# Encoder trunk on one core: three stage boundaries rearranged (a transposition bank for one gate product, the first statistics, the odd mixer's constant rows)

## The chip, the cores and the metric

The kernel runs on one core of a Trainium2 chip. The core has five engines with a queue of instructions each: TensorE (PE, matrix products), VectorE (DVE), ScalarE (ACT), GpSimd (POOL) and SyncE (SP, which here only issues DMAs). Each engine works through its queue in order; semaphores make an instruction wait for another engine or a DMA. The metric is device time in microseconds (us) of one execution, lower is better. Every time in this text is in us unless it says otherwise.

## The reference

The reference is a two-layer encoder on 512 tokens of width 1024, all in fp32:

```python
for i in range(DEPTH):                       # DEPTH = 2
    h = h + 0.5 * swiglu(rmsnorm(h, norm_ffn1[i]), ffn1_w_gate[i], ffn1_w_up[i], ffn1_w_down[i])
    hn = rmsnorm(h, norm_mix[i])
    if i % 2 == 0:
        h = h + ab_mixer(hn, ...)            # windowed and dilated attention
    else:
        h = h + c_mixer(hn, ...)             # 2-D neighbourhood attention, 16 heads of 64
    h = h + 0.5 * swiglu(rmsnorm(h, norm_ffn2[i]), ffn2_w_gate[i], ffn2_w_up[i], ffn2_w_down[i])
    gate = jax.nn.sigmoid(rmsnorm(h, norm_ple[i]) @ w_ple_gate[i])
    h = h + gate * (p[i] @ w_ple_proj[i])    # per-layer input embedding
return rmsnorm(h, norm_final)
```

`rmsnorm` multiplies by `rsqrt(mean(x*x) + 1e-6)` and a gain; `swiglu` is `(silu(x @ w_gate) * (x @ w_up)) @ w_down` with 2816 inner columns. In the odd layer's mixer the 512 tokens are a grid 64 wide, and each query sees 8 rows by 16 columns around it.

## The kernel before, in words

**Layout.** The residual stream lies transposed: eight chunks (`KC = 8`) of 128 features by 512 tokens (`T = 512`). A weight *unit* is 128x1024 values, the weights of one block of 128 outputs over all eight chunks.

**Products.** An fp32 product is made of three matmuls (`mm3`, L175 to L177): high part by high part, high weight by low data, low weight by high data. A unit is loaded by SP into one of five raw buffers (`wr`), ACT copies its high part into `wh` (L150) and DVE subtracts to get the low part `wl` (L151), four buffers each. So a product of one unit over 512 tokens is 24 matmuls into one PSUM bank.

**PSUM.** There are eight banks in four pools: three `mm` (`bank`), two `sc` (`sbank`), two `tr` (`tbank`, for transpositions, column sums and the spread of the norm factor) and one `ob` (`obank`). A pool gives its banks out in turn; a new use waits for the readers of the old one.

**Norms.** The products run on the unnormalised data times the gain, and the factor 1/rms is multiplied in afterwards. ACT squares each chunk (L219), DVE adds the squares up (L226), PE sums over the partitions by products with a column of ones (`stat`, L233), DVE scales (L235), POOL takes the power -1/2 (L236), PE spreads the result over all partitions by four transposes (`spread`, L252), and ACT copies it into the tile `R` (L260). `rcol` and `R` are properties: whoever asks first puts that work at this place of the program.

**Stages.** Each layer runs FFN 1, the mixer, FFN 2 and the embedding stage (`ple`). In the FFN, `pair_front` makes the first four pairs of gate and up products (L294 to L297 are what follows them), `pair` the fifth, and a faster scheme (L390 to L392 on PE) the others. The first FFN of the program is special: it starts while x is still loading. For its first pair (m == 0) the units of the second pair are asked for ahead (`self.ahead`), then all eight squares and sums are issued, and R.

**The embedding stage** has eight chunks. The first three gate products are made ahead of R: m = 0 and m = 1 in `mm` banks with their projections in `ob` and `sc`, then m = 2 in the third `mm` bank (`ahead`); rcol and R come in the middle and at the end of it. From m = 3 on a gate product takes the next `mm` bank, and its projection (6 matmuls) an `sc` bank. DVE multiplies the gate by R (L1387), ACT takes the sigmoid (L1388), DVE multiplies with the projection (L1389) and adds to the stream (L1395 or L1412).

**The odd mixer** (`c`) starts with four sets of constant rows: eight tiles (`sel`, `low`) of which half the partitions hold a constant (64x512), brought by four DMAs into temporary tiles (L1201) and rounded by POOL (L1203). Then come the first q and k, the first v (`project_v`, L759 to L761, L778), and a weave of *steps* (the softmax and the P-V product of each of the sixteen heads, two to a pair) and *fill* (the projections of later pairs). L705 and L717 are ACT's copies that stack q and k by halves; q's are then copied by DMA into the free half of `sel` (L1233). L1301 are the scores, L1311 and L1317 the exponential and the normalisation, L791 the transposes of P, L801 and L802 the P-V product.

**What sets the order.** The program is written in one order, and a planner puts the instructions of each engine in the order in which, by its own costs, they can start. `issue_after` makes an instruction start behind a named one, `keep_in_program_order` ties a list, and `high_priority` draws a block ahead.

Of the kernel before, what the change touches and what calls it, by code (L numbers as in the profile page):

```python
# [15 lines left out]
P = 128  # L16
# [17 lines left out]
FRONT = 4  # L34
WHOLE = 4
# [13 lines left out]
class Trunk:  # L49
# [99 lines left out]
    def split(self, src, hi, lo, lo_eng=None):  # L149
        self.put(self.nc.scalar.activation(hi, src, AF.Copy))  # L150
        self.put((lo_eng or self.nc.vector).tensor_tensor(lo, src, hi.bitcast(F32), op=ALU.subtract))  # L151
# [64 lines left out]
    def norm_square(self, c):  # L216
        nc = self.nc
        sq = self.tmp() if c else self.small("ssq", [P, T], bufs=1)
        ins = nc.scalar.activation(sq, self.h[c], AF.Square)  # L219
        if self.k == 0:  # L220
            self.tc.keep_in_program_order(ins)
        if c == 0:
            self.acc = sq
        else:
            eng = nc.vector if c == KC - 1 or self.k in (0, 1, 3, 5, 7) else nc.gpsimd
            self.last_sum = eng.tensor_tensor(self.acc, self.acc, sq, op=ALU.add)  # L226

# [36 lines left out]
    def pair_front(self, w, m, first, ahead):  # L264

        nc = self.nc
        pgu = [self.bank(), self.sbank()]
        for j in range(2):
            u = self.ahead.pop(0) if self.ahead else self.unit(
                w[:, (1 - j) * UNIT:(2 - j) * UNIT], behind=self.last_sum if first and m == 2 else None)  # L270
            if not (first and m == 0):
# [12 lines left out]
        if m == 0 and first:  # L284

            with ExitStack() as s:
                for ins in self.last:
                    s.enter_context(self.tc.issue_after(ins.ins))
                self.ahead = [self.unit(ahead[:, (1 - j) * UNIT:(2 - j) * UNIT]) for j in range(2)]
            for c in range(KC):  # L290
                self.norm_square(c)
# [8 lines left out]
    def mm_pair(self, p, u, xs, j, ks=range(KC)):  # L300

        for k in ks:
            c = (k + KC // 2 * j) % KC * P
            self.mm3(p, (u[0][:, c:c + P], u[1][:, c:c + P]), xs[k], k == 0, k == KC - 1)
# [886 lines left out]
    def c(self, k_next):  # L1191
# [5 lines left out]
        for hf in range(2):  # L1197
            free = slice((1 - hf) * HD, (2 - hf) * HD)
            for name, dst in (("sel_c", sel), ("mask_c", low)):
                t = self.tmp()  # L1200
                nc.sync.dma_start(t[free, :], io[name])  # L1201
                for i in range(2):
                    nc.gpsimd.tensor_copy(dst[i][hf][free, :], t[free, :])  # L1203
# [52 lines left out]
        vs[0] = self.project_v(io["v_c"][0], nat, lambda: self.rcol, banks=[self.sbank(), self.bank()])  # L1256
        fill, steps = [], []
# [87 lines left out]
    def ple(self, i, k_next, regroup):  # L1345
# [4 lines left out]
        for m in range(KC):  # L1350
# [23 lines left out]
            for x in (slice(0, T // 2), slice(T // 2, T)) if half else (slice(0, T),):  # L1374
# [3 lines left out]
                else:  # L1378
                    pg, pp = (ahead if m == 2 else self.bank())[:, x], self.sbank()[:, x]
# [210 lines left out]
```

## Time and profile before

| | us |
|---|---|
| median of 3 runs | 2018.9 |
| lowest, highest | 2018.16, 2019.87 |
| profiled execution, its own time | 2018.84 |
| its span, first to last instruction | 2017.0 |
| PE busy | 1995.4 (99%) |
| DVE busy | 1593.9 (79%) |
| ACT busy | 1126.0 (56%) |
| POOL busy | 271.2 (13%) |

The granted clock of PE was 0.998 over the span. In a timeline each row gives the start, the length, the engine, the line and operation, output and inputs with their shapes, the count of merged instructions, and in brackets the idle time ahead of it with what ended it. A matmul's row is longer than the step to the next, since they overlap; the step is read from the starts. In a table of waits a row gives who waited for whom, the total in us, the number of times, and the longest.

### The profile page before, as it was taken

The page shows a single profiled execution, that of the slowest core. Times are in us where ns is not written, and L with a number is a line of the kernel's source. Part 1 is how long each engine was busy: PE and PEld are TensorE (multiplying, and loading weights), DVE is VectorE, ACT ScalarE, POOL GpSimd, SP SyncE. Part 2 cuts the span into 40 slices and gives each one's busy share as a digit, 9 for nine tenths or more (in the row PEclk, how much of TensorE's full clock was granted, in tenths as well). Part 3 has the DMA queues.
Part 4 walks back from the last instruction along what each step waited for, and adds up shares of the span by engine and source line. Part 5 has one row for each costly group of instructions (what it writes and reads, how often), then busy time and mean ns, then how long its engine had stood idle before and what let it go on. Part 6 is the DMA issues. An engine that isn't in the chain of part 4 may idle for free.

```text
span 2017.0 us, 33409 instructions
## 1 busy us (share of the span) xinstructions
PE 1995.4 (99%) x12438; PEld 1782.9 (88%) x12438; DVE 1593.9 (79%) x2803; ACT 1126.0 (56%) x1954; POOL 271.2 (13%) x314
## 2 busy tenths in 40 slices
PE   9999999999999999999999999999999999999997
PEld 6999988878888899988788999888988889998886
DVE  7888976798766888896778888958888678889675
ACT  6455655477644455575554555745766545556543
POOL 0000021342212000012120000113000100001211
PEclk9999999999999999999999999999999999999999
DMA  6666697643425466689554666885343446667971
GB/s 198 178 186 180 199 210 216 177 94 75 102 71 167 115 177 185 172 226 220 197 167 126 184 178 183 228 203 186 105 133 103 157 115 165 178 180 213 222 229 42
DMA packets 134963, 334.94 MB, mean 166 GB/s; under 512 B 24592, under 2 KB 32272, under 8 KB 134800
## 3 DMA queue, kind: packets, MB, share of 16 engines
q1 hardware_dynamic: 106944, 245.72, 36.0%
q0 software_dynamic: 27712, 87.05, 24.4%
q8 instruction: 98, 1.61, 0.3%
q14 instruction: 65, 0.53, 0.1%
q10 hardware_dynamic: 144, 0.04, 0.0%
HBM read 304.42 MB, written 17.27 MB: 159 GB/s over the span
## 4 chain that ended last, share of the span: by engine, by line
PE 75%; DVE 3%; ACT 2%; issue 1%; DMA 0%; POOL 0%; DVEq 0%; ACTq 0%; POOLq 0%
PE mm L176 5%; PE mm L175 5%; PE mm L177 5%; PE mm L391 5%; PE mm L392 5%; PE mm L390 5%; PE sc L390 2%; PE sc L392 2%; PE sc L391 2%; PE mm L511 2%; PE mm L509 2%; PE mm L510 2%; PE sc L175 2%; PE sc L177 2%; PE sc L176 2%; PE sc L511 1%
## 5 line engine op out<-in xcount | busy, mean ns | idle before, releaser
L150 ACT ACTIVATE wh<-wr 128x1024 fp32r<-128x1024 f32 (+2 forms) x435 | 447.9, 1031 | 428.0 <-PE mm L176 75.6
L151 DVE TENSOR_TENSOR wl<-wr,wh 128x1024 fp32r<-128x1024 f32 (+2 forms) x435 | 521.2, 1200 | 158.1 <-ACT wh L150 154.9
L390 PE MATMUL mm<-act,wh 128*128 128x256 f32 x1088 | 307.9, 283 | 0.0
L392 PE MATMUL mm<-act,wl 128*128 128x256 f32 x1088 | 307.9, 283 | 0.0
L391 PE MATMUL mm<-act,wh 128*128 128x256 f32 x1088 | 307.9, 283 | 0.0
L175 PE MATMUL mm<-act,wh 128*128 128x512 f32 (+1 forms) x632 | 248.0, 394 | 2.4 <-DVE tmp L1387 2.0
L176 PE MATMUL mm<-act,wh 128*128 128x512 f32 (+1 forms) x632 | 247.3, 392 | 0.7 <-DVE act L214 0.6
L177 PE MATMUL mm<-act,wl 128*128 128x512 f32 (+1 forms) x632 | 246.5, 391 | 0.0
L390 PEld LDWEIGHTS mm<-act,wh 128*128 128x128 f32 x1088 | 208.9, 192 | 0.2
L391 PEld LDWEIGHTS mm<-act,wh 128*128 128x128 f32 x1088 | 208.9, 192 | 0.2
L392 PEld LDWEIGHTS mm<-act,wl 128*128 128x128 f32 x1088 | 208.9, 192 | 0.0
L392 PE MATMUL sc<-act,wl 128*128 128x256 f32 x544 | 154.0, 283 | 0.0
L390 PE MATMUL sc<-act,wh 128*128 128x256 f32 x544 | 154.0, 283 | 0.0
L391 PE MATMUL sc<-act,wh 128*128 128x256 f32 x544 | 154.0, 283 | 0.0
L368 POOL DMA_DIRECT2D wr<-in_gu_dram x68 | 59.2, 870 | 677.2 <-DMA wr<-in_gu_dram 272.2
L175 PEld LDWEIGHTS mm<-act,wh 128*128 128x128 f32 x632 | 118.8, 188 | 26.0 <-DVE tmp L1387 2.9
L176 PEld LDWEIGHTS mm<-act,wh 128*128 128x128 f32 x632 | 118.9, 188 | 24.5 <-DVE act L214 3.3
L177 PEld LDWEIGHTS mm<-act,wl 128*128 128x128 f32 x632 | 118.9, 188 | 21.3
L500 POOL DMA_DIRECT2D wr<-in_dn_dram x80 | 69.2, 873 | 405.8 <-DVE wl L151 278.2
L151 DVE TENSOR_TENSOR act<-act,act 128x512 fp32r<-128x512 f32 (+1 forms) x176 | 108.3, 628 | 8.1 <-ACT act L150 5.6
L150 ACT ACTIVATE act<-act 128x512 fp32r<-128x512 f32 (+1 forms) x176 | 98.5, 577 | 16.9 <-DVE act L151 6.7
L390 PEld LDWEIGHTS sc<-act,wh 128*128 128x128 f32 x544 | 104.5, 192 | 0.0
(254 smaller groups left out, 4864.9 us busy)
## 6 DMA issues: line engine op xcount, KB each, us to landing
wr<-in_gu_dram SPq DMA_DIRECT2D x176, 512.0 KB, 4.2
wr<-in_gu_dram POOLq DMA_DIRECT2D x68, 512.0 KB, 5.4
wr<-in_dn_dram POOLq DMA_DIRECT2D x64, 512.0 KB, 7.1
tmp<-in_dn_dram SPq DMA_DIRECT2D x120, 256.0 KB, 4.7
rb<-in_gu_dram SPq DMA_DIRECT2D x68, 256.0 KB, 2.5
wr<-in_dn_dram SPq DMA_DIRECT2D x32, 512.0 KB, 4.6
act<-kept SPq DMA_DIRECT2D x56, 256.0 KB, 5.2
wr<-in_qk_ab_dram SPq DMA_DIRECT2D x20, 512.0 KB, 3.5
```

What stands on the lines that cost most here:

```text
L150: self.put(self.nc.scalar.activation(hi, src, AF.Copy))
L151: self.put((lo_eng or self.nc.vector).tensor_tensor(lo, src, hi.bitcast(F32), op=ALU.subtract))
L175: mm(out, stat[0], mov[0], start=start, stop=False)
L176: mm(out, stat[0], mov[1], start=False, stop=False)
L177: return mm(out, stat[1], mov[0], start=False, stop=stop)
L368: nc.gpsimd.dma_start(rs, w[:, :UNIT], accum_op=ALU.add)
L390: mm(out, w[0][:, c], xs[k][0][:, x], start=start and k == 0, stop=False, skip_group_check=True)
L391: mm(out, w[0][:, c], xs[k][1][:, x], start=False, stop=False, skip_group_check=True)
L392: mm(out, w[1][:, c], xs[k][0][:, x], start=False, stop=stop and k == half - 1, skip_group_check=True)
L500: nc.gpsimd.dma_start(raw, b[:, u.start * T:u.stop * T], accum_op=ALU.add)
L509: mm(p, xh, wh, start=start and k == 0, stop=False, skip_group_check=True)
L511: ins = mm(p, xl, wh, start=False, stop=stop and k == u.stop - 1, skip_group_check=True)
```

## The change

There are three edits.

**First statistics.** Of the second pair's units only the gate's is asked for ahead of the squares; the up unit's split is put behind the last square. The squares of the chunks behind `SQ_FIRST = 4` are tied behind the gate unit's high part. The second pair's gate product is started inside the first call of `pair_front` in two halves of 12 matmuls, with rcol between them and R behind the second; the second call takes it over (`self.started`).

**Embedding stage.** The gate product of m == 3 takes a `tr` bank.

**Odd mixer.** The constants are loaded and rounded behind the first v, by ACT.

```diff
@@ split, norm_square, mm_pair: what they keep or return
-        self.put(self.nc.scalar.activation(hi, src, AF.Copy))
+        self.last_hi = self.put(self.nc.scalar.activation(hi, src, AF.Copy))
...
+        return ins
...
-            self.mm3(p, (u[0][:, c:c + P], u[1][:, c:c + P]), xs[k], k == 0, k == KC - 1)
+            self.last_mm = self.mm3(p, (u[0][:, c:c + P], u[1][:, c:c + P]), xs[k], k == 0, k == KC - 1)
@@ pair_front
-        pgu = [self.bank(), self.sbank()]
+        pgu = [None if first and m == 1 else self.bank(), self.sbank()]
...
-            if not (first and m == 0):
+            if first and m == 1 and j == 0:
+                pgu[0] = self.started
+            elif not (first and m == 0):
                 self.mm_pair(pgu[j], u, self.xg, j)
...
-                self.ahead = [self.unit(ahead[:, (1 - j) * UNIT:(2 - j) * UNIT]) for j in range(2)]
+                self.ahead = [self.unit(ahead[:, UNIT:])]
+                hi = self.last_hi
             for c in range(KC):
-                self.norm_square(c)
+                with self.tc.issue_after(hi.ins) if c > SQ_FIRST else ExitStack():
+                    square = self.norm_square(c)
+            self.ahead.append(self.unit(ahead[:, :UNIT], behind=square))
+            self.started, half = self.bank(), KC // 2
+            self.mm_pair(self.started, self.ahead[0], self.xg, 0, range(half))
+            with self.tc.issue_after(self.last_mm.ins):
+                self.rcol
+            self.mm_pair(self.started, self.ahead[0], self.xg, 0, range(half, KC))
+            with self.tc.issue_after(self.last_mm.ins):
+                self.R
@@ c
-        for hf in range(2):
-            free = slice((1 - hf) * HD, (2 - hf) * HD)
-            for name, dst in (("sel_c", sel), ("mask_c", low)):
-                t = self.tmp()
-                nc.sync.dma_start(t[free, :], io[name])
-                for i in range(2):
-                    nc.gpsimd.tensor_copy(dst[i][hf][free, :], t[free, :])
+        def constants():
+            for hf in range(2):
+                free = slice((1 - hf) * HD, (2 - hf) * HD)
+                for name, dst in (("sel_c", sel), ("mask_c", low)):
+                    t = self.tmp()
+                    nc.sync.dma_start(t[free, :], io[name])
+                    for i in range(2):
+                        nc.scalar.activation(dst[i][hf][free, :], t[free, :], AF.Copy)
...
         vs[0] = self.project_v(io["v_c"][0], nat, lambda: self.rcol, banks=[self.sbank(), self.bank()])
+        constants()
@@ ple
-                    pg, pp = (ahead if m == 2 else self.bank())[:, x], self.sbank()[:, x]
+                    g = ahead if m == 2 else self.tbank() if m == 3 else self.bank()
+                    pg, pp = g[:, x], self.sbank()[:, x]
```

In the changed kernel's rows the line numbers are larger by one from L35 on, and by more further down (L176 to L178 for `mm3`, L151 and L152 for the split, L1219 for the constants).

The first place is DVE's queue around the first sums, in the first FFN. `wl_239` before and `wl_262` after are the low half of the second pair's up unit; `wl_404` and `wl_434` belong to the third pair, `wl_500` to the fourth pair's gate, and L294 (after: L308) is the first product with R. Before:

```order
L151 TENSOR_TENSOR wl_233<-wr_231,wh_232 128x1024
L151 TENSOR_TENSOR wl_239<-wr_237,wh_238 128x1024
L226 TENSOR_TENSOR ssq_243<-ssq_243,tmp_245 128x512
...
L226 TENSOR_TENSOR ssq_243<-ssq_243,tmp_263 128x512
L151 TENSOR_TENSOR wl_404<-wr_402,wh_403 128x1024
L235 TENSOR_SCALAR ms_272<-tr_267 128x4
L151 TENSOR_TENSOR wl_434<-wr_432,wh_433 128x1024
L898 TENSOR_SCALAR sink_3947<-sink_3947 128x12
L294 TENSOR_TENSOR tmp_282<-mm_181,R_266 128x512
```

and after:

```order
L152 TENSOR_TENSOR wl_233<-wr_231,wh_232 128x1024
L227 TENSOR_TENSOR ssq_237<-ssq_237,tmp_239 128x512
...
L227 TENSOR_TENSOR ssq_237<-ssq_237,tmp_254 128x512
L152 TENSOR_TENSOR wl_262<-wr_260,wh_261 128x1024
L227 TENSOR_TENSOR ssq_237<-ssq_237,tmp_257 128x512
L152 TENSOR_TENSOR wl_404<-wr_402,wh_403 128x1024
L237 TENSOR_SCALAR ms_284<-tr_279 128x4
L152 TENSOR_TENSOR wl_434<-wr_432,wh_433 128x1024
L912 TENSOR_SCALAR sink_3947<-sink_3947 128x12
L152 TENSOR_TENSOR wl_500<-wr_498,wh_499 128x1024
L308 TENSOR_TENSOR tmp_307<-mm_181,R_300 128x512
```

The up unit's low half has moved from ahead of the seven sums to ahead of the last of them, and `wl_500`, which stood 34 rows behind the first product with R, stands ahead of it. On ACT the split of the up unit follows the squares, and the high half of the same fourth pair's gate (`wh_499`) stands ahead of the copy of R.

The second place is DVE's queue in the first layer's embedding stage, around the third chunk (m = 2). The two low halves are those of the gate units of m = 5 and m = 6. Before:

```order
L151 TENSOR_TENSOR wl_11258<-wr_11256,wh_11257 128x1024
L214 SCALAR_TENSOR_TENSOR act_11105<-act_11100,gain,act_11104 128x512
L1387 TENSOR_TENSOR tmp_11120<-mm_11037,R_11071 128x512
L151 TENSOR_TENSOR wl_11314<-wr_11312,wh_11313 128x1024
L1389 TENSOR_TENSOR tmp_11121<-sc_11113,tmp_11120 128x512
```

and after:

```order
L152 TENSOR_TENSOR wl_11258<-wr_11256,wh_11257 128x1024
L152 TENSOR_TENSOR wl_11314<-wr_11312,wh_11313 128x1024
L215 SCALAR_TENSOR_TENSOR act_11105<-act_11100,gain,act_11104 128x512
L1405 TENSOR_TENSOR tmp_11120<-mm_11037,R_11071 128x512
L1407 TENSOR_TENSOR tmp_11121<-sc_11113,tmp_11120 128x512
```

The second low half has moved ahead of the gate's product with R. PE's order there is unchanged but for the bank: the 24 matmuls of m = 3 write `tr_11144` in place of `mm_11144`.

The third place is ACT's queue behind the copy of R in the odd mixer. Before:

```order
L260 ACTIVATE R_15430<-tr_15431 128x512
L778 ACTIVATE act_15417<-mm_15290,rcol_15351 128x4x64
L705 ACTIVATE act_15440<-tmp_15429 64x512
...
L717 ACTIVATE act_15454<-tmp_15448 64x512
L150 ACTIVATE wh_15884<-wr_15883 128x1024
L150 ACTIVATE wh_15938<-wr_15937 128x1024
L1311 ACT_TABLE_LOAD
```

and after:

```order
L262 ACTIVATE R_15430<-tr_15431 128x512
L792 ACTIVATE act_15401<-mm_15274,rcol_15335 128x4x64
L1219 ACTIVATE act_15170<-tmp_15404 64x512
...
L1219 ACTIVATE act_15177<-tmp_15416 64x512
L719 ACTIVATE act_15440<-tmp_15429 64x512
...
L731 ACTIVATE act_15454<-tmp_15448 64x512
L151 ACTIVATE wh_15884<-wr_15883 128x1024
L151 ACTIVATE wh_15938<-wr_15937 128x1024
L151 ACTIVATE wh_16045<-wr_16044 128x1024
L1328 ACT_TABLE_LOAD
```

The eight copies of the constants now stand between R and the copies that stack q and k, and one more split stands ahead of the first exponential. On PE the first scores (L1301, after: L1318) stand 18 rows further down, behind 11 matmuls of the second pair's k; some 350 rows further on the orders are alike again.

More of the change, by code (lines that the diff above doesn't have):

```diff
@@ L34 @@
 FRONT = 4
+SQ_FIRST = 4
 WHOLE = 4
```

## The prediction

> **What bounds the kernel now.** Read first is the page's table of busy time, then the waits of PE alone, then the timeline at the three places that the change touches. Lines are those of the kernel before.
>
> ```profile
> PE 1995.4 (99%) x12438; PEld 1782.9 (88%) x12438; DVE 1593.9 (79%) x2803; ACT 1126.0 (56%) x1954; POOL 271.2 (13%) x314
> ```
>
> PE is busy 1995.4 of 2017.0 us, so only what shortens PE's row or takes an idle stretch out of it moves the end. Idle stretches are few (total in us, times, longest):
>
> ```profile
> PE mm L175 <- DVE tmp L1387: 2.0, 2, 1.0
> PE tr L233 <- DVE ssq L226: 1.3, 2, 0.7
> PE ob L801 <- ACT tmp L150: 1.2, 5, 0.3
> PE tr L252 <- POOL rcol L236: 0.8, 1, 0.8
> ```
>
> The first, second and fourth rows are what the three edits aim at: 4.1 us together as the waits count them. No edit takes work from PE, so the gain is these stretches and the slow restart behind each, less what becomes late next.
>
> **First statistics.** PE's row, before (start, length, instruction, idle ahead of it):
>
> ```profile
> 22.81 0.39 PE L176 MATMUL mm<-act,wh 128*128 128x512 f32 x1
> 23.89 1.05 PE L233 MATMUL tr<-ones,ssq 128*128 128x1 f32 x8 [0.69 <-DVE ssq L226]
> 24.80 0.48 PE L177 MATMUL mm<-act,wl 128*128 128x512 f32 x1
> ...
> 26.03 0.39 PE L176 MATMUL mm<-act,wh 128*128 128x512 f32 x1
> 27.21 0.65 PE L252 MATMUL tr<-ident,rcol 128*128 128x128 f32 x4 [0.79 <-POOL rcol L236]
> 27.61 0.48 PE L177 MATMUL mm<-act,wl 128*128 128x512 f32 x1
> ...
> 29.31 0.39 PE L175 MATMUL sc<-act,wh 128*128 128x512 f32 x1
> ```
>
> A 512-column matmul lasts 0.39 in the model but they follow each other every 0.23 (24.80 to 26.03 is five steps, the first of 0.32). So PE stood from 23.04 to 23.89 for the sum of squares and from 26.26 to 27.21 for the power on POOL: 0.85 + 0.95 = 1.80. The change lets the statistic come after 12 matmuls of the second pair's gate instead of 11, and the four transposes after all 24. When is the sum ready?
>
> ```profile
> 16.14 1.06 ACT L150 ACTIVATE wh<-wr 128x1024 fp32r<-128x1024 f32 x1 [0.22 <-DMA wr<-in_gu_dram]
> 17.63 3.74 ACT L219 ACTIVATE tmp<-act 128x512 f32<-128x512 f32 x7
> 15.95 2.51 DVE L151 TENSOR_TENSOR wl<-wr,wh 128x1024 fp32r<-128x1024 f32 x2 [0.68 <-ACT wh L150]
> 18.38 5.46 DVE L226 TENSOR_TENSOR ssq<-ssq,tmp 128x512 f32<-128x512 f32 x7
> 24.98 0.16 DVE L235 TENSOR_SCALAR ms<-tr 128x4 f32<-128x4 f32 x1
> 25.22 1.93 POOL L236 TENSOR_TENSOR rcol<-ms,mhalf 128x4 f32<-128x4 f32 x1 [24.78 <-DVE ms L235]
> ```
>
> The second unit's split moves behind the squares: ACT drops 1.06 ahead of them, so squares pace nothing. On DVE one subtraction (2.51/2 = 1.25) goes out ahead of the first sum, which then starts near 17.1; six sums of 0.78 (5.46/7) end at 21.8; the moved subtraction now stands between the sixth and the seventh and costs 1.2; the seventh sum (0.7) ends near 23.7, against 23.84. The statistic can start at 23.75, PE is there at 23.27: 0.48 idle. Statistic 0.91 (24.80 - 23.89), twelve matmuls 2.8, so PE reaches the transposes at 27.5. They need the power, which came 3.32 behind the statistic (27.21 - 23.89): 27.07, no wait. Transposes 0.40, and the up product begins at 27.9 instead of 29.31; 0.09 goes on its slow first step. **Gain 1.35**; bounds 0.6 (the moved subtraction a whole 0.8 later than I place it) and 1.8 (both stretches gone).
>
> What is late next? The spread R on ACT now stands behind a fourth split that waits for PE to leave its buffer at about 27.3, so R ends near 28.9, and one subtraction stands ahead of the first product with R. DVE has no room from there on:
>
> ```profile
> 30.00:60.00 30.00, 30.00 (x139) 25.02 (x138) 29.98 (x57) 16.86 (x29) 1.96 (x2) 1.00 0.54 106
> 28.53 0.69 DVE L294 TENSOR_TENSOR tmp<-mm,R 128x512 f32<-128x512 f32 x1 [2.16 <-ACT R L260]
> 49.92 1.21 DVE L151 TENSOR_TENSOR wl<-wr,wh 128x1024 fp32r<-128x1024 f32 x1
> 51.77 0.39 PE L177 MATMUL sc<-act,wl 128*128 128x512 f32 x1
> ```
>
> DVE is busy 29.98 of these 30 us (third figure). The low half that ends at 51.1 is first used at 51.77: 0.6 to spare, and PE now comes about 1.4 earlier. But the subtraction ahead (1.2) leaves the dense stretch, and two shorter operations (0.9) now stand behind this low half. DVE's first product with R moves from 28.53 to about 29.6: +1.0 - 1.2 - 0.9 = 1.1 earlier. That is short of what PE gained by 0.3 and covered by the 0.6. I take 0.1 off, 1.25 for the part; if DVE gets none of its own time back, the part is worth 0.3.
>
> **Embedding stage, both layers.** The fourth product's gate waited for the first product's bank:
>
> ```profile
> 1004.16 0.40 PE L177 MATMUL sc<-act,wl 128*128 128x512 f32 x1
> 1005.56 0.50 PE L175 MATMUL mm<-act,wh 128*128 128x512 f32 x1 [1.00 <-DVE tmp L1387]
> 1005.90 0.39 PE L176 MATMUL mm<-act,wh 128*128 128x512 f32 x1
> ...
> 1969.59 0.50 PE L175 MATMUL mm<-act,wh 128*128 128x512 f32 x1 [1.00 <-DVE tmp L1387]
> 1003.55 0.58 ACT L260 ACTIVATE R<-tr 128x512 f32<-128x512 f32 x1
> 1016.32 0.68 DVE L1389 TENSOR_TENSOR tmp<-sc,tmp 128x512 f32<-128x512 f32 x1
> 1017.95 0.39 PE L175 MATMUL sc<-act,wh 128*128 128x512 f32 x1
> ```
>
> Free of that bank it starts at 1004.39 rather than 1005.56, and the restart step shrinks from 0.34 to 0.23: 1.28. The transposition bank is free once ACT has copied R, at 1004.13, 0.26 ahead. The second layer has the same rows: **2.56 together**; bounds 0 (R's copy, or the bank's other user, later than the old wait) and 2.56. Late next is the fifth projection: PE wants its bank at 1016.66 instead of 1017.95, and L1389 must have read it. Before it ended at 1017.0. In the new order on DVE both coming low halves are made ahead of it, but the first of them started when PE left the fourth gate (now 1.28 earlier), so I place its end at 1016.0 to 1016.5: just enough. I take off 0.1: 2.45.
>
> **Constants.** POOL's casts lie beside DVE's sums:
>
> ```profile
> 1388.03 1.22 DVE L151 TENSOR_TENSOR wl<-wr,wh 128x1024 fp32r<-128x1024 f32 x1
> 1389.76 1.63 DVE L151 TENSOR_TENSOR wl<-wr,wh 128x1024 fp32r<-128x1024 f32 x1
> 1393.47 3.12 DVE L226 TENSOR_TENSOR ssq<-ssq,tmp 128x512 f32<-128x512 f32 x3
> 1393.05 4.01 POOL L1203 CAST act<-tmp 64x512 fp32r<-64x512 f32 x4 [1.18 <-DMA tmp<-in_sel_c_dram]
> 1395.81 0.28 PE L761 MATMUL mm<-wh,act 128*128 128x256 f32 x1
> 1396.74 1.02 PE L233 MATMUL tr<-ones,ssq 128*128 128x1 f32 x8 [0.65 <-DVE ssq L226]
> 1397.63 0.36 PE L759 MATMUL sc<-wh,act 128*128 128x256 f32 x1
> ```
>
> Beside casts a subtraction takes 1.63, else 1.22; a sum of three takes 3.12, at the first stage's 0.78 each it would be 2.34. The last three alone give 0.8, the earlier pieces another 1, so the sum ends by 1395.7 and the statistic starts at 1395.93: 0.81 idle and 0.08 of slow restart go, **0.87**; bounds 0 (the slowness has another cause) and 0.89.
>
> By the Trainium skill (SBUF - State Buffer, "Who interferes with whom") a vector instruction with two SBUF inputs and a GpSimd instruction that reads SBUF exclude each other for a whole instruction. The trace agrees in direction, not in size: 0.41 is lost beside casts of 1.0 to 1.3. By the rule in full the sums would end several us earlier still, and the term would stay 0.87, since PE's own place caps it.
>
> The cost is on ACT: eight copies of 64x512, between
>
> ```profile
> 1408.41 1.27 ACT L705 ACTIVATE act<-tmp 64x512 fp32r<-64x512 f32 x2
> 1419.82 0.51 ACT L1311 ACTIVATE act<-act,st_c 128x256 f32<-128x256 f32 x1 [2.61 <-DVE st_c L1305]
> 1418.68 1.12 PE L1301 MATMUL sc<-act,act 128*128 128x256 f32 x8
> ```
>
> 0.53 (a square above) and 0.64 (L705) each: 4.2 to 5.1, ahead of the copies that stack the first q and k, hence of their DMAs and of the first scores (1418.68). The planner has put 18 fill matmuls, 18 x 0.23 = 4.1, ahead of those scores, and ACT has 2.61 idle ahead of its first exponential. So PE works on; at worst 0 to 1.0 is uncovered. The four loads keep their neighbours in SP's queue; what stands behind them is needed by ACT only after 1403. I take 0.
>
> **Sum.** 1.25 + 2.45 + 0.87 = 4.57 off the profiled execution's 2018.84 (span 2017.0 and 1.8 around it), which lies 0.1 under the median of 2018.9: 2014.3.
>
> **Rivals.** (1) *DVE sets the end of the first FFN's front.* For: 29.98 of 30 us. Against: the subtraction drawn ahead. Then part one keeps 0.3: 2018.84 - 0.3 - 2.45 - 0.87 = 2015.2; if the moved subtraction also makes the statistic late, 2015.6. (2) *The odd mixer pays for its constants once.* The first scores' operands land up to 1.0 late, or the 18 matmuls used early are missing behind a later softmax, up to 4.1. For: ACT works in order, and nothing shows the DMAs' slack. Against: PE's order is as before again some 350 rows on. Taking 2.0: 2016.3. (3) *The odd mixer pays in every half-head*: slower. The shifted weave lets a stacking copy (0.63) of the next pair stand ahead of the exponentials or the normalisation in each of the 14 half-heads left, and PE's transposes wait each time: 14 x 0.63 = 8.8, so 2018.84 - 3.70 + 8.8 = 2023.9. It outweighs the other gains from 0.27 per half-head. For: PE already waits for ACT at L801, five times. Against: 0.3 at most, and ACT is busy 56%. (4) *The tr bank is no freer than the old one*: part two nothing, 2016.7; the 0.26 ahead of need speaks against it.
>
> **How the numbers follow.** Forecast 0.55, (1) 0.17, (2) 0.15, (3) 0.07, (4) 0.06. Time: 2014.3. The forecast's own bounds are 2013.7 (part one 1.8) to 2015.2. The range goes down to 2013.0, for stretches nearby that shrink too, and up over (1), (2) and (4) to 2017.6; left out is (3) and a little on each side. About 0.2% (4.0 us) is what a measurement of this kernel can tell from no change: faster is below 2014.9, slower above 2022.9. The forecast lies only 0.5 inside: 0.8 of it and a tenth of (1) and (2) count as faster, with a little for smaller waits that vanish unasked: 0.52. Slower is (3), 0.07; the rest, 0.41, is no measurable change.
>
> **What would show it.** In the changed profile PE's waits should have lost the row for L1387's bank altogether; the first statistic's wait should shrink to about 0.4 and that of the first transposes vanish; the odd mixer's statistic should start some 0.1 behind the matmul ahead of it, with its last three sums in 2.4. PE's busy time should stay, its idle fall by over 4. A wait of PE for a low half between 30 and 60 us would be (1); a new wait at the scores, the transposes or L801 in the odd mixer (2) or, repeated, (3); a wait for ACT's R at the fourth gate (4). The forecast is wrong if idle time returns elsewhere, or if the sums in the odd mixer are as slow without casts.

## The result and the profile after

The changed kernel took 2015.44 us in the median (2014.98 to 2017.61, 20 runs) against 2019.39 (2017.55 to 2021.08, 20 runs) for the kernel before: a ratio of 0.9984, 95% interval 0.9977 to 0.9991. By the ratio that is 3.2 us less, by its interval 1.8 to 4.6. The execution that was profiled is the slowest of the 20: 2017.61, with a span of 2015.8. It has a stretch of 3.4 us at half clock, which is told of at the end; a second profile of the same kernel has none.

The page of the changed kernel, its busy times, and some rows of the waits of PE (total in us, times, longest):

```profile
PE 1996.1 (99%) x12438; PEld 1784.5 (89%) x12438; DVE 1590.0 (79%) x2803; ACT 1131.1 (56%) x1962; POOL 262.0 (13%) x306
```

```profile
PE mm L177 <- DVE act L215: 0.9, 3, 0.3
PE tr L235 <- DVE ssq L227: 0.8, 1, 0.8
...
PE ob L816 <- DVE tmp L152: 0.7, 2, 0.4
...
PE mm L773 <- DVE tmp L1255: 0.6, 1, 0.6
```

The rows for the embedding stage's first bank (2.0 before) and for the power at the first transposes (0.8) are gone; the sum of squares is waited for once, not twice. New is `mm L773 <- DVE tmp L1255`, and the rows for L215 and L816 have grown (0.6 and 0.4 before). They are three places at which something came late next.

**First statistics.** PE, then DVE, of the changed kernel:

```profile
21.94 0.39 PE L178 MATMUL mm<-act,wl 128*128 128x512 f32 x1
23.11 1.05 PE L235 MATMUL tr<-ones,ssq 128*128 128x1 f32 x8 [0.78 <-DVE ssq L227]
...
26.63 0.39 PE L178 MATMUL mm<-act,wl 128*128 128x512 f32 x1
26.86 0.60 PE L254 MATMUL tr<-ident,rcol 128*128 128x128 f32 x4
27.21 0.48 PE L176 MATMUL sc<-act,wh 128*128 128x512 f32 x1
```

```profile
16.65 4.67 DVE L227 TENSOR_TENSOR ssq<-ssq,tmp 128x512 f32<-128x512 f32 x6
21.23 1.22 DVE L152 TENSOR_TENSOR wl<-wr,wh 128x1024 fp32r<-128x1024 f32 x1
22.37 0.69 DVE L227 TENSOR_TENSOR ssq<-ssq,tmp 128x512 f32<-128x512 f32 x1
```

The transposes follow the matmul ahead of them without a wait, and from the statistic to the up product are 4.10 (23.11 to 27.21) where the kernel before had 5.42 (23.89 to 29.31). PE still stands 0.93 ahead of the statistic, for the seventh sum, which waits behind the moved subtraction (21.23). The lead is kept: the transposes of the FFN's second norm started at

```profile
374.09 0.60 PE L252 MATMUL tr<-ident,rcol 128*128 128x128 f32 x4
```

before, and in the changed kernel at

```profile
372.09 0.60 PE L254 MATMUL tr<-ident,rcol 128*128 128x128 f32 x4
```

**Embedding stage**, first layer, PE, and PE at the end of the stretch, where the next FFN's front begins:

```profile
1004.35 0.39 PE L178 MATMUL sc<-act,wl 128*128 128x512 f32 x1
1004.58 0.39 PE L176 MATMUL tr<-act,wh 128*128 128x512 f32 x1
...
1044.16 0.50 PE L177 MATMUL mm<-act,wh 128*128 128x512 f32 x1 [0.28 <-DVE act L215]
```

The fourth gate follows after one step of 0.23. But 40 us on PE waits for DVE's low half of an x chunk (L215), 0.28, which the kernel before did not do there.

**Odd mixer.** DVE's last three sums, then PE at the statistic:

```profile
1391.69 2.14 DVE L227 TENSOR_TENSOR ssq<-ssq,tmp 128x512 f32<-128x512 f32 x3
```

```profile
1395.07 0.28 PE L775 MATMUL mm<-wh,act 128*128 128x256 f32 x1
1395.19 0.95 PE L235 MATMUL tr<-ones,ssq 128*128 128x1 f32 x8
```

Three sums take 2.14 instead of 3.12, and the statistic stands 0.12 behind the matmul ahead of it. Behind it ACT makes the copies:

```profile
1406.89 4.39 ACT L1219 ACTIVATE act<-tmp 64x512 fp32r<-64x512 f32 x8
1411.19 1.27 ACT L719 ACTIVATE act<-tmp 64x512 fp32r<-64x512 f32 x2
```

They take 4.39, inside the 4.2 to 5.1 of the prediction. What they cost is the subject of the experiments.

To compare where the time went, PE's row is divided at the transposes of each norm (their start is in the same rows as 374.09 and 372.09) and, in the odd mixer, at the statistics. Of the stretches not listed, the one with the even mixer varies by chance (280.8 to 281.6, and 283.1 and 283.3 in two executions, see the end), the one behind the final statistic by up to 0.6, and the others agree within 0.1. The 0.6 goes with the clock: the granted clock falls to half near the end of every execution, 6.9 behind the final statistic in the two profiles in which that stretch is 16.7 long (the half-late kernel and the change's second), and 7.4 to 10.0 behind it in the other eight, in which it is 16.1 to 16.3.

| stretch, us | before | change | first statistics alone | bank alone | constants alone |
|---|---|---|---|---|---|
| first statistic to the up product behind the first transposes | 5.42 | 4.10 | 4.11 | 5.44 | 5.42 |
| from that up product to the second norm's transposes | 344.78 | 344.88 | 344.92 | 344.80 | 344.78 |
| embedding stage, first layer | 49.30 | 48.38 | 49.27 | 48.40 | 49.30 |
| next FFN to the odd mixer's transposes | 351.59 | 350.69 | 351.61 | 351.60 | 350.69 |
| odd mixer's transposes to the next statistic | 209.37 | 211.08 | 209.33 | 209.33 | 211.13 |
| embedding stage, second layer | 34.24 | 32.95 | 34.25 | 33.31 | 34.28 |

The last three columns are the first experiments. The edits add: each moves its own stretches and no other.

### The profile page after: what moved, and what is told of

It reads as the page before. It is cut to its first block, busy times and chain, and to the rows that moved or that the text cites. A ratio compares the mean times of both kernels' runs of the same rounds, so it can differ in the third digit from the quotient of the medians.

```text
span 2015.8 us, 33406 instructions
## 1 busy us (share of the span) xinstructions
PE 1996.1 (99%) x12438; PEld 1784.5 (89%) x12438; DVE 1590.0 (79%) x2803; ACT 1131.1 (56%) x1962; POOL 262.0 (13%) x306
## 4 chain that ended last, share of the span: by engine, by line
PE 76%; DVE 2%; ACT 1%; issue 1%; POOL 0%; DVEq 0%; ACTq 0%; POOLq 0%
PE mm L177 5%; PE mm L176 5%; PE mm L178 5%; PE mm L406 5%; PE mm L405 5%; PE mm L404 5%; PE sc L406 2%; PE sc L405 2%; PE sc L404 2%; PE mm L523 2%; PE mm L524 2%; PE mm L525 2%; PE sc L176 2%; PE sc L177 2%; PE sc L178 2%; PE sc L523 1%
## 5 line engine op out<-in xcount | busy, mean ns | idle before, releaser
L151 ACT ACTIVATE wh<-wr 128x1024 fp32r<-128x1024 f32 (+2 forms) x435 | 447.6, 1032 | 427.9 <-PE mm L177 75.6
L152 DVE TENSOR_TENSOR wl<-wr,wh 128x1024 fp32r<-128x1024 f32 (+2 forms) x435 | 519.4, 1196 | 160.9 <-ACT wh L151 157.5
L176 PE MATMUL mm<-act,wh 128*128 128x512 f32 (+1 forms) x616 | 242.2, 395 | 0.8 <-ACT act L214 0.5
L177 PE MATMUL mm<-act,wh 128*128 128x512 f32 (+1 forms) x616 | 241.5, 393 | 0.9 <-DVE act L215 0.9
L178 PE MATMUL mm<-act,wl 128*128 128x512 f32 (+1 forms) x616 | 241.0, 392 | 0.0
L176 PEld LDWEIGHTS mm<-act,wh 128*128 128x128 f32 x616 | 116.3, 189 | 22.8 <-ACT act L214 1.1
L178 PEld LDWEIGHTS mm<-act,wl 128*128 128x128 f32 x616 | 116.2, 189 | 20.9 <-DVE wl L152 0.2
L152 DVE TENSOR_TENSOR act<-act,act 128x512 fp32r<-128x512 f32 (+1 forms) x176 | 108.4, 629 | 8.0 <-ACT act L151 5.8
L151 ACT ACTIVATE act<-act 128x512 fp32r<-128x512 f32 (+1 forms) x176 | 98.5, 577 | 16.9 <-DVE act L152 6.7
```

The lines of the kernel that those rows point to most:

```text
L151: self.last_hi = self.put(self.nc.scalar.activation(hi, src, AF.Copy))
L176: mm(out, stat[0], mov[0], start=start, stop=False)
L177: mm(out, stat[0], mov[1], start=False, stop=False)
L178: return mm(out, stat[1], mov[0], start=False, stop=stop)
```

## The experiments

### Each edit alone

```diff
# first statistics alone: pair_front, split, norm_square as in the change; ple and c as before
# bank alone: the kernel before with
+                    g = ahead if m == 2 else self.tbank() if m == 3 else self.bank()
+                    pg, pp = g[:, x], self.sbank()[:, x]
# constants alone: the kernel before with constants() behind the first v, on ScalarE
```

> Only the first statistics are changed; the bank and the constants are as before. Reading of the two profiles: the change's statistic still waits 0.78 for the last sum, its transposes no longer wait, and the lead of 2.1 at the up product's start is still 2.0 at 62 us; but 1.1 of it was there before the statistics (the first weights landed earlier). So I expect 1.0 to 1.4 off the time of before (ratio 0.9993 to 0.9995), PE waiting 0.4 to 0.8 at the statistic, none at the transposes, and no wait for a low half between 30 and 62 us. Rival (DVE sets the end of this stretch): the lead at the up product's start is gone by 62 us and the time is as before within 0.3.

> Only the fourth gate product's bank is changed. Expected: no wait for L1387's bank, 1.28 off in each embedding stage less up to 0.3 in the first, 2.2 to 2.5 off in all (ratio 0.9988). Rival (the waits behind it take it back in the first layer): 1.3 off, and a new wait at a projection or in the FFN behind the first embedding stage.

> Only the constants are moved: to ScalarE, behind the first v. Theory: 0.9 is won at the odd mixer's statistic and 1.6 is lost in the weave, since the planner draws 18 fill matmuls ahead of the first scores, and one lap later three waits stand at the P-V product and at v's product (its bank not yet read by DVE); from the mixer's R transposes to the next statistic 211.1 against 209.4 before. In all 0.7 slower than before (ratio 1.0003). Rival (the loss in the weave belongs to another edit, or is chance): 0.9 faster, and that stretch takes 209.4.

Measured on the same chip (before: 2018.59, 31 runs): first statistics alone 2017.66, ratio 0.9993 (0.9985 to 1.0002); bank alone 2016.89, 0.9991 (0.9982 to 0.9999); constants alone 2019.88, 1.0001 (0.9992 to 1.0010). By the timings alone only the bank is told from nothing. The stretches of the table tell more, since the loading at the start and what varies by chance elsewhere lie outside them: first statistics -1.31 + 0.14 = -1.2, bank -0.90 - 0.93 = -1.8, constants -0.90 + 1.76 = +0.9. So the constants' edit, which was to gain 0.87, gains that and loses twice as much in the weave behind it. The bank's 1.8 lies between what was expected (2.2 to 2.5) and its rival (1.3): the wait in the next FFN that the rival named is there (0.28), but takes back only a part of the first layer's gain.

One thing the table leaves out is when the first statistic comes. It starts at 23.89 before and 23.11 in the change, but the constants alone, where nothing ahead of it is changed, has

```profile
9.90 1.16 ACT L150 ACTIVATE wh<-wr 128x512 fp32r<-128x512 f32 x2 [0.45 <-DMA wr<-in_gu_dram]
```

```profile
23.15 1.05 PE L233 MATMUL tr<-ones,ssq 128*128 128x1 f32 x8 [0.75 <-DVE ssq L226]
```

and the kernel before has that pair of splits, of the first up weights, 0.77 later:

```profile
10.67 1.15 ACT L150 ACTIVATE wh<-wr 128x512 fp32r<-128x512 f32 x2 [1.39 <-DMA wr<-in_gu_dram]
```

From this row to the statistic it is 13.22, 13.31 and 13.25 in the three profiles without the new statistics, and 12.93 to 13.58 (mean 13.25) in the six with them. So the edit does not bring the first statistic forward; it puts one more matmul ahead of it, and the wait there falls from 0.69, 0.81 and 0.75 to between 0.22 and 0.78 (mean 0.49). The weights came between 9.90 and 10.67 in the former and between 9.53 and 9.95 in the latter; whether the edit has a hand in that is open.

### The constants at the old place, on ScalarE

```diff
+        constants()
         first = [self.obank(), self.bank()]
         self.mm_units(first, [self.unit(io["qk_c"][i], lo_eng=self.lo_eng()) for i in range(2)])
         vs[0] = self.project_v(io["v_c"][0], nat, lambda: self.rcol, banks=[self.sbank(), self.bank()])
-        constants()
```

> All three edits, but the constants are rounded on ScalarE at their old place in the program, ahead of the first q and k products, so that the eight copies fall into ScalarE's idle time behind the squares, and the planner's weave is that of before. Theory: the statistic keeps its 0.9, the stretch from the mixer's R transposes to the next statistic is back at 209.4, and the time is 1.6 under the changed kernel's, about 2014.0 where that has 2015.4 (ratio to before 0.9975). Rival (the loss comes from ScalarE's extra 4.4 us wherever they stand): the time is the changed kernel's, with the waits elsewhere in the mixer.

Measured: 2014.58 (9 runs), ratio 0.9976 (0.9966 to 0.9986). From the odd mixer's transposes to the next statistic it is 209.31, the 209.37 of before, and the gain ahead of it is kept (350.68). ACT makes the copies in gaps between squares and splits:

```profile
1385.37 1.15 ACT L1219 ACTIVATE act<-tmp 64x512 fp32r<-64x512 f32 x2
...
1389.02 2.20 ACT L1219 ACTIVATE act<-tmp 64x512 fp32r<-64x512 f32 x4
```

and DVE's sums beside them are as fast as without any (1.41 for two):

```profile
1390.24 1.41 DVE L227 TENSOR_TENSOR ssq<-ssq,tmp 128x512 f32<-128x512 f32 x2
```

So the engine alone brings the 0.90, and the place is what costs the 1.77 (211.08 - 209.31). POOL's casts at the late place were not run. By this stretch the kernel is 1.77 under the change; the two were not timed beside each other, and the intervals of their ratios overlap.

### What in the late place costs it: half the copies late

```diff
-        def constants():
+        def constants(names):
...
-                for name, dst in (("sel_c", sel), ("mask_c", low)):
+                for name, dst in names:
...
+        constants([("sel_c", sel)])
         first = [self.obank(), self.bank()]
...
-        constants()
+        constants([("mask_c", low)])
```

> All three edits, but only four of the eight constant copies (the mask) stand late on ScalarE, the other four (the selector) at the old place. The planner now draws 9 fill matmuls ahead of the first scores where the changed kernel draws 18. Theory (fill used early is missing behind a later softmax): the stretch from the mixer's R transposes to the next statistic is 0.5 to 1.2 longer than the 209.3 with none late, between that and 211.1 with all late. Rival (the loss is one fixed misfit of the planner's order, or comes with the scores' operands): 209.3 or 211.1, or more, whatever is drawn ahead.

### The change once more, beside the half

> The changed kernel itself, unedited, beside the other two on one chip, and for a second profile. In the first profile PE's granted clock was 0.52 from 545.2 to 548.7, which is not in any of the other five profiles and cost about 1.5. Theory: that is chance, the second profile lacks it, and its stretches read 1.7 off in the first stage, 0.9 and 0.9 to 1.3 off in the two embedding stages, 0.9 off at the odd mixer's statistic and 1.75 lost in the weave. Rival (it belongs to the changed kernel): it stands there again.

Measured (before: 2018.92, 24 runs): half late 2016.98, ratio 0.9989 (0.9980 to 0.9998); the change again 2015.89, 0.9983 (0.9975 to 0.9992). The profiled execution of the former has the chance stretch at half clock, that of the latter has not. In the weave the half costs 210.91 - 209.37 = 1.54 over the kernel before, the whole 211.08 - 209.37 = 1.71. The half was not half: 1.60 over the old place is outside the 0.5 to 1.2 of the theory and nearer to the rival, so neither the number of copies nor the number of fill matmuls drawn ahead of the first scores (9 rows and 18) sets the price in proportion. The change's second profile repeats the stretches of the first: the embedding stages 0.93 and 1.28 off, the odd mixer's front 0.92 off, the weave 1.71 lost; the first stage, from the statistic to the second norm's transposes, is 1.22 off, not the 1.7 expected.

### The copies behind the stacking copies

```diff
         def soft(hp, hf):
+            if hp + hf == 0:
+                constants()
...
-        constants()
```

> All three edits, with the eight copies of the constants still on ScalarE and still behind the first v, but written behind the products of the first q and k with R, so that ACT's queue has the copies that stack k and q (L719, L731) in between and ahead of most of the constants. PE's order has the first scores 4 rows lower than the kernel before, where the change has them 18 lower. ACT carries the same eight copies (4.4 us) in the same stretch. Stretch from the R transposes of the odd mixer to the next statistic: 209.3 with the constants early, 211.1 in the change. Theory 1 (what the change loses comes from the stacking copies of the first q and k standing behind the eight copies: the scores go lower, and DVE stands idle behind ACT's L719 early in the weave and is missing later): 209.3 to 209.9. Theory 2 (4.4 us more on ACT ahead of the first exponential costs the same wherever they stand, since the softmax is late by them): 210.6 to 211.2. Whole time by theory 1 about 2014.5, by theory 2 about 2016; all the other stretches as in the change.

Measured: 2016.85 (10 runs) against 2018.62, ratio 0.9991 (0.9981 to 1.0). The weave takes 212.17: worse than the change, by more than either theory said. Theory 1, that the first pair's stacking behind the copies is the harm, has fallen: here the stacking is early and so are the scores, and the loss is larger. On ACT another place has filled:

```profile
1418.61 2.18 ACT L1219 ACTIVATE act<-tmp 64x512 fp32r<-64x512 f32 x4
1420.81 1.28 ACT L1329 ACT_TABLE_LOAD   x1
```

Four of the copies now stand right ahead of the table load and the first exponential. That suggests to order the kernels by when the first softmax runs. Start of the transposes on PE, of the first exponential on ACT and of the next statistic on PE; the kernel with the constants at the old place:

```profile
1399.36 0.60 PE L254 MATMUL tr<-ident,rcol 128*128 128x128 f32 x4
1415.72 0.51 ACT L1328 ACTIVATE act<-act,st_c 128x256 f32<-128x256 f32 x1 [2.61 <-DVE st_c L1322]
1608.67 0.95 PE L235 MATMUL tr<-ones,ssq 128*128 128x1 f32 x8
```

half late:

```profile
1401.64 0.60 PE L254 MATMUL tr<-ident,rcol 128*128 128x128 f32 x4
1421.17 0.51 ACT L1329 ACTIVATE act<-act,st_c 128x256 f32<-128x256 f32 x1 [0.33 <-DVE st_c L1323]
1612.55 0.95 PE L235 MATMUL tr<-ones,ssq 128*128 128x1 f32 x8
```

the change:

```profile
1401.82 0.60 PE L254 MATMUL tr<-ident,rcol 128*128 128x128 f32 x4
1422.26 0.51 ACT L1328 ACTIVATE act<-act,st_c 128x256 f32<-128x256 f32 x1 [1.25 <-DVE st_c L1322]
1612.90 0.95 PE L235 MATMUL tr<-ones,ssq 128*128 128x1 f32 x8
```

behind the stacking:

```profile
1399.85 0.60 PE L254 MATMUL tr<-ident,rcol 128*128 128x128 f32 x4
1422.11 0.51 ACT L1329 ACTIVATE act<-act,st_c 128x256 f32<-128x256 f32 x1
1612.02 0.95 PE L235 MATMUL tr<-ones,ssq 128*128 128x1 f32 x8
```

All four in one table, in us, lateness and loss against the old place:

| | first scores behind the transposes | first exponential behind them | lateness of the exponential | weave | loss | loss / lateness |
|---|---|---|---|---|---|---|
| old place | 15.2 | 16.36 | 0 | 209.31 | 0 | |
| half late | 17.3 | 19.53 | 3.17 | 210.91 | 1.60 | 0.50 |
| change | 19.3 | 20.44 | 4.08 | 211.08 | 1.77 | 0.43 |
| behind the stacking | 16.1 | 22.26 | 5.90 | 212.17 | 2.86 | 0.48 |

The loss follows the start of the first exponential, at 0.43 to 0.50 of its lateness, and not that of the first scores, which are nearly on time in the last row. Three late orders are few, and they differ in more than this: it is an order that fits, not a cause shown. Why half of it is made good again in the weave was not tried. PE does not wait for the exponentials at first, since it has fill to do. In the changed kernel DVE stands idle behind ACT at the weave's start,

```profile
1411.84 1.41 DVE L720 TENSOR_TENSOR act<-tmp,act 64x512 fp32r<-64x512 f32 x2 [3.07 <-ACT act L719]
...
1419.74 1.22 DVE L152 TENSOR_TENSOR wl<-wr,wh 128x1024 fp32r<-128x1024 f32 x1 [2.07 <-ACT wh L151]
```

and some 18 us later PE waits for DVE:

```profile
1437.93 0.39 PE L816 MATMUL ob<-tmp,act 128*128 128x256 f32 x1 [0.34 <-DVE tmp L152]
...
1439.44 0.39 PE L773 MATMUL mm<-wh,act 128*128 128x256 f32 x1 [0.55 <-DVE tmp L1255]
```

Here are the 40 us from the transposes on, of the change and of the kernel with the constants at the old place (the window, the sum, then busy time and instructions of PE, PEld, DVE, ACT and POOL):

```profile
1401.82:1441.82 40.00, 39.03 (x236) 34.20 (x234) 29.62 (x80) 29.98 (x64) 0.00 (x0) 1.00 0.41 114
```

```profile
1399.36:1439.36 40.00, 40.00 (x250) 35.74 (x249) 33.09 (x91) 28.32 (x63) 0.00 (x0) 1.00 0.44 123
```

DVE is busy 29.62 against 33.09, PE loses 0.97 in waits and gets through 236 matmuls against 250. In the kernel with the copies behind the stacking the wait is another one, for the exponential itself, 1.40 ahead of a P-V product at 1436.95.

Such waits are not the whole loss. Over the whole weave, the kernel with the constants at the old place and the half-late kernel:

```profile
1399.36:1608.67 209.31, 208.12 (x1230) 182.28 (x1229) 164.68 (x422) 136.51 (x295) 9.02 (x6) 1.00 0.41 124
```

```profile
1401.64:1612.55 210.91, 209.80 (x1230) 182.28 (x1229) 164.18 (x422) 139.14 (x299) 9.00 (x6) 1.00 0.41 123
```

PE has the same matmuls and stands idle 1.19 and 1.11 (sum less busy): the half-late kernel loses 1.60 with no more idle time at all, by longer steps between matmuls, which the profile counts as busy since a matmul's row is longer than its step. In the change PE is idle 1.97, 0.78 of its 1.77; behind the stacking 2.39, 1.20 of its 2.86. Counted by steps beyond the usual one of each kind of matmul (its median at the old place), 1.05 (half late), 1.62 (change) and 2.33 (behind the stacking) of the losses fall between 20 and 40 us behind the transposes, most of the rest between 40 and 60, and nothing later. So the place of the loss is known; what makes the steps longer there no run takes apart.

### The last sum no longer behind the split

With the constants at the old place, the up unit's low half is put behind the last sum, and the third pair's splits behind the scaling of the statistic:

```diff
-        nc.vector.tensor_scalar(ms[:, :n], ps[:, :n], 1.0 / D, EPS, op0=ALU.mult, op1=ALU.add)
+        self.ms = nc.vector.tensor_scalar(ms[:, :n], ps[:, :n], 1.0 / D, EPS, op0=ALU.mult, op1=ALU.add)
...
-                w[:, (1 - j) * UNIT:(2 - j) * UNIT], behind=self.last_sum if first and m == 2 else None)
+                w[:, (1 - j) * UNIT:(2 - j) * UNIT], behind=self.ms if first and m == 2 else None)
...
-            self.ahead.append(self.unit(ahead[:, :UNIT], behind=square))
+            raw, uhi, ulo = self.unit_tiles()
+            nc.sync.dma_start(raw, ahead[:, :UNIT])
+            with self.tc.issue_after(square.ins):
+                nc.scalar.activation(uhi, raw, AF.Copy)
+            with self.tc.issue_after(self.last_sum.ins):
+                nc.vector.tensor_tensor(ulo, raw, uhi.bitcast(F32), op=ALU.subtract)
+            self.ahead.append((uhi, ulo))
```

> The kernel of the run before (all edits, constants at their old place) with one more step in the first stage: the up unit's low half is subtracted behind the seventh sum instead of ahead of it, and the third pair's splits stand behind the scaling of the statistic, so that POOL's power starts as soon as the sums are in. Theory: the statistic waits for the last sum because a 1.2 subtraction stands in DVE's queue ahead of it; without it the wait of 0.8 is gone or under 0.1, PE reaches the transposes 0.7 earlier and finds the power ready; 0.6 to 0.8 off against that run, about 2013.9 where it has 2014.6 (ratio to before 0.9972). Rival (DVE has no room up to 62 us, so a lead won here is not kept): the up product begins earlier, but by 62 us the lead is that of the run before.

Measured: 2013.41 (2013.04 to 2014.77, 8 runs) against 2018.92, ratio 0.9972 (0.9962 to 0.9982): the fastest version here, 2.5 under the change beside it; its slowest run lies under the fastest of the change's 11. DVE and PE:

```profile
16.27 5.46 DVE L227 TENSOR_TENSOR ssq<-ssq,tmp 128x512 f32<-128x512 f32 x7
```

```profile
22.42 0.95 PE L235 MATMUL tr<-ones,ssq 128*128 128x1 f32 x8
...
371.35 0.60 PE L254 MATMUL tr<-ident,rcol 128*128 128x128 f32 x4
```

All seven sums run through, the statistic waits for nothing, and the second norm's transposes come at 371.35, where the six profiles with the change's own statistics have 371.83 to 372.22 (mean 372.02): 0.67, inside the 0.6 to 0.8 expected. So the lead is kept, against the rival.

## Why the prediction was right, and where it was wrong

The time said was 2014.3, 4.57 less than a profiled 2018.84; measured is 3.2 less by the ratio (1.8 to 4.6), with a median of 2015.44. That is inside the range, but outside the forecast's own bounds (2013.7 to 2015.2), and the range is wide because it was stretched over the rivals: the hit alone does not confirm the forecast. The interval lies clear of no change, yet 0.16% is less than the 0.2% that the prediction took as the least it could tell, so by its own line this is "no measurable change", which it gave 0.41, and not "faster", which it gave 0.52. The direction held, and so did four of five terms, one of them by three quarters; one term of nothing should have been 1.7. By stretches of the trace (the weave from the change's second profile):

| term | predicted | measured |
|---|---|---|
| first statistics | -1.25 | -1.32 + 0.10 = -1.22 |
| embedding stage, first layer | -1.23 | -0.92 |
| embedding stage, second layer | -1.23 | -1.29 (or -0.93) |
| odd mixer, up to the transposes | -0.87 | -0.90 |
| odd mixer, the weave | 0 | +1.71 |
| sum | -4.57 | -2.6 |

The -2.6 of these stretches and the 3.2 of the timings agree within the interval; where the rest lies is not known.

**First statistics: right step by step.** From the statistic to the up product the prediction has 4.15 (23.75 to 27.9), the change 4.10: the wait at the transposes is gone entirely. At the statistic it takes off 0.14, of which the runs show nothing. The 0.1 that it gives back is the +0.10 of the next stretch.

**Rival (1), DVE sets the front's end, did not happen.** DVE is again busy throughout,

```profile
30.00:60.00 30.00, 30.00 (x145) 25.28 (x145) 30.00 (x58) 16.96 (x29) 1.96 (x2) 1.00 0.54 103
```

yet PE's lead at the up product (2.10) is still there at the second norm (2.00). PE made 145 matmuls in these 30 us, where it had made 139. The step that placed DVE's relief (two short operations gone, a subtraction drawn ahead) held. The 0.3 that the rival was said to leave is not worked out from a row; the row it rests on has 0.6 to spare.

**Embedding stage: right bank, one late follower overlooked.** The tr bank was free, as said, so rival (4) is out, and the fifth projection came without a wait:

```profile
1016.08 0.69 DVE L1407 TENSOR_TENSOR tmp<-sc,tmp 128x512 f32<-128x512 f32 x1 [0.70 <-ACT tmp L1406]
```

It ends at 1016.77, a little behind the 1016.0 to 1016.5 that were given (this profile runs 0.18 behind that of before here), and PE's first matmul into its bank starts at 1017.05. But the term stopped there. In the first layer the stage is followed by an FFN whose front works on x chunks that DVE makes last (L215); with PE 1.2 ahead, DVE's low half is 0.28 late, and that and its restart are the 0.3 missing. The bank alone has the same 0.28, so it is this edit's. In the second layer the full 1.29 was paid in the change, and 0.93 where the final statistic waited 0.54 instead of 0.17 for POOL's sum; why the latter happens in two of the profiles is open.

**Constants: the gain right, the price wrong.** The 0.87 and its mechanism held: without casts the sums take 2.14 for three (the prediction said 2.4) and PE's own place caps the gain. By the Trainium skill (SBUF - State Buffer, "Who interferes with whom") PE and ACT never wait for anyone at these ports. ACT's copies agree: four beside DVE's sums at the old place take 2.20, four with no sum beside them, behind the stacking, 2.18. The sums lose nothing either (1.41 for two, the same per sum as in the first stage or better).

The step that failed is "So PE works on; at worst 0 to 1.0 is uncovered ... I take 0". It costed ACT's 4.4 by PE alone at the first scores, where indeed PE never waits: the 18 fill matmuls cover them. It left out what stands behind the copies on ACT. DVE stood idle behind ACT, the first exponential came 4.08 late, and 20 to 40 us behind the transposes PE lost 1.6, of which 0.9 are waits for DVE. Nor were the 2.61 that ACT stood idle ahead of its first exponential room for the copies: the row says that ACT waited there for DVE's `st_c`, which waits for the scores, and 1.25 of this wait are still there in the change. The prediction had the price as rival (2), that the mixer pays once, at 2.0; measured is 1.7. Its chance of 0.15 was too low: the point *for* the rival, that ACT works in order, decided, and the point against, "PE's order is as before again some 350 rows on", says only that the order recovers and not the time. But neither of the two ways that the rival named is shown: nothing waits at the first scores, and the matmuls used early do not set the price, since 9 of them cost 1.60, 18 cost 1.77, and with 4 the loss was 2.86. It is paid once: groups of P-V products that start 77.2, 138.1 and 171.4 behind the transposes before start at 78.9, 139.9 and 173.1 in the change's second profile, 1.7 to 1.8 later throughout, so rival (3) is out.

**The signs named.** L1387's row is gone, the transposes wait for nothing, the odd statistic stands 0.12 behind its predecessor, the sums take 2.14: four as said. The first statistic's wait, said to shrink to about 0.4, is 0.78 in the first profile and 0.22 in the second. PE's idle (span less busy time) was to fall by over 4 and fell by 1.9, from 21.6 to 19.7: part of it came back as the waits at L773, L816 and L215.

## What to carry to other kernels

Cover at the place of a move is not enough. A moved block also delays everything behind it on the engine that it occupies, so ask how late that engine's first work for the next stage becomes, even where the engine that bounds the kernel is covered at the move itself. Here the loss was about half of the first exponential's lateness, in three orders of one kernel. Where an engine ahead is idle (ACT among the squares), put the block there; the change of engine and the change of place are two edits, and here one gained 0.90 and the other lost 1.7. And when a wait at a boundary is removed, look for the next consumer well behind it, not only for the next user of the same bank.

## What the runs showed of the hardware

The profiled execution of the change has a stretch in which the granted clock was about half (windows: PE busy is the second figure behind the window, the clock the third from the end):

```profile
541.70:545.20 3.50, 3.26 (x26) 2.72 (x24) 3.38 (x13) 2.29 (x10) 1.26 (x2) 1.00 0.67 74
545.20:548.70 3.50, 3.50 (x10) 2.77 (x10) 2.86 (x12) 1.66 (x7) 0.00 (x0) 0.52 0.34 132
```

Eight matmuls follow each other there every 0.43 instead of 0.23:

```profile
546.18 0.63 PE L177 MATMUL mm<-act,wh 128*128 128x512 f32 x1
546.61 0.63 PE L178 MATMUL mm<-act,wl 128*128 128x512 f32 x1
```

The half clock lasts 3.41, from 545.33 on. The half-late kernel's profile has the same stretch at the same place (clock 0.51), the other eight profiles, the change's second one among them, have none. It costs about 2: from the second to the third norm's transposes it takes 283.28 and 283.10 with it, 280.8 to 281.6 without. So a single profile of one kernel can mislead by 2 us, which is as much as the largest part of this change. By the Trainium skill (TensorE: Matmul & The Clock Gate, "Part 1: The HAM clock gate") the clock is at half after at least one idle window of some 3.4 us. The length of the stretch agrees; an idle window ahead of it is not to be seen, since by the profile's rows PE was busy 3.26 of the 3.5 before. The cause stays open. In both executions the sixteen short score products ahead of it start at 542.07 and 542.36, in the others at 541.10 to 541.92 or at 543.23 to 543.74; whether that phase matters was not tried.
